# Sums of a fast matrix product kept in PSUM and read between their terms, in the feed-forward layer of a decoder step

## The chip, the cores and the metric

The kernel runs on one core of a Trainium2 chip. The metric is the device time of one execution in microseconds (us). A core has five engines that run their own instruction streams and wait for each other by semaphores: TensorE (PE, matrix products into PSUM), VectorE (DVE), ScalarE (ACT), GpSimd (POOL) and SyncE (SP, which here issues loads).

## The reference, cut to what matters

One decoder layer on 512 prompt rows and 8 x 4 sample rows, 544 token columns in all, in float32. Only its last part is touched by the change:

```python
x += SwiGLU(RMSNorm(x))              # D_MODEL 2048, FFN_HIDDEN 5632
def swiglu(h, w_gate, w_up, w_down):
    return (jax.nn.silu(h @ w_gate) * (h @ w_up)) @ w_down
y = rmsnorm(x, norm_final_w)
```

Ahead of it stand the token mixer (a recurrent group and a sliding-window attention) and a memory cross-attention, which take the first 1137 us of the span and are the same before and after.

## The kernel before

**Units.** The three feed-forward products are made in units by a fast scheme with 7 products in place of 8. Weights and activations are cut into 2 x 2 blocks; `unit` (L1642) loads the four weight blocks A11, A21, A12, A22 by two DMAs of 1 MB on SP (tile `sraw`) and POOL makes three combinations S1, S2, S3 and later a fourth (tile `scomb`, 3 buffers, `comb` at L1655). The 7 products come in the order B11, B21, T2, T1, T3, B22, T4, named by the activation block that each multiplies. There are 44 units of gate and up (22 pairs; the weight block is 8 row tiles by one column tile) and then 20 units of w_down: 5 blocks `b` of hidden rows by 4 groups `o4` of output columns. The last 4 of the 44 row tiles of hidden values go through the plain product `gemm` at the end.

**Products.** Each product is 24 matmuls of 128 x 272 (L1692): the weights are split in a high part `shi` and a low part `slo`, the activations too, and high x high, high x low, low x high are added in PSUM. `split_w2` (L1634) makes the parts: ACT copies the source to a PSUM tile `h2` (rounded; L1638; "h" in the rows), ACT casts the source to `shi` (L1639), and DVE subtracts `h2` from the source into `slo` (L1640). `shi` and `slo` have two buffers each, so those of product q+2 can be written only when PE has ended product q; `h2` has one buffer (two banks), so a copy waits for the DVE subtraction of the product before. The 24 matmuls need `slo` first at their third.

**Results.** Each product has a PSUM tile of its own (`s_ps`, pool `ps_acc`, 2 buffers of 2 banks each; T1's is in `ps_s`), and `done` reads it out:

- gate and up (`gu_unit`, L1701): ACT copies B11's result twice (L1712, L1713), and DVE adds and subtracts the other six into the four result blocks (8 instructions of 272 columns, L611 and L1699), with four multiplications by the norm factor in a gate unit (L1706).
- w_down (`down_unit`, L1875): B11, T2, T1 and T3 go into sums of their own in SBUF (`sums`): ACT copies in block 0 (L1884), DVE adds from block 1 on; B21, B22 and T4 are added by DVE straight to `x`. In the last block 32 more additions of 544 columns (`x_sum`, L1862, its instruction at L1870) bring the sums into `x`: those of one `o4` in the unit after it, from the unit's hook, and those of the last in its own `done`, partly on POOL.

**Activation operands.** The split operands of the w_down blocks are made beside the units: `Block.early` (in the unit before the block, o4 = 3) and `Block.late` (in the block's first unit, o4 = 0). POOL forms the differences (L1756), ACT casts the high part (L606), DVE subtracts it for the low part (L607; two inputs in SBUF, 1088 columns). In the last block's second unit `last_h` splits the 4 row tiles that are left (L607, 544 columns).

**Order.** Within one engine the instructions stand in the order that the program's builder gives them when it places them by its own estimate of readiness, so the order of a line in the source is not always the order on the engine: `h2` and `shi` of one product, which the source writes in that order, can stand either way round on ACT.

Of the kernel before, what the change touches and what calls it, by code (L numbers as in the profile page):

```python
# [19 lines left out]
P = 128  # L20
# [24 lines left out]
def hybrid_step(ctx: ExitStack, tc: tile.TileContext, a):  # L45
# [13 lines left out]
    ps_s = pool("ps_s", bufs=2, space=PSUM)  # L59
# [4 lines left out]
    def ps(name, tag="t"):  # L64
        return (ps_s if tag == "s" else ps_to[0]).tile([P, 512], F32, tag=tag, name=name)
# [1156 lines left out]
    def norm_rows(out, sums, tag="t"):  # L1222

        for (b, e), s in zip(HALF, sums):
            pt = ps("nr_ps", tag)[:, : TT // 2]
# [404 lines left out]
    to_ctx.close()  # L1630
    ph_ctx = ctx.enter_context(ExitStack())
    ps_h = ph_ctx.enter_context(tc.tile_pool(name="ps_h", bufs=1, space=PSUM))

# [8 lines left out]
    def unit(w1, w2, n0, m, ops, done, hook=None, loaded=None, summed=None):  # L1642
# [23 lines left out]
        if summed:  # L1666
            with tc.issue_after(last.ins):
                summed()
        for i, (q, src) in enumerate((
# [3 lines left out]
            if src is None:  # L1673
                src, _ = comb(A12, S2, SPLIT)
# [21 lines left out]
            done(q, accs if q == "T1" else acc[:, :m, :HT])  # L1696
# [4 lines left out]
    def gu_unit(w, n0, c, f, *more):  # L1701
# [6 lines left out]
        def done(q, acc):  # L1708
            c11, c12, c21, c22 = (c[:, i, t] for i in range(2) for t in (T0, T1))
            acc = acc[0] if q == "T1" else acc[:, 0]  # L1710
# [23 lines left out]
        held = []  # L1734
        unit(*w, n0, 1, fops.get, done, *more)


# [69 lines left out]
    for j in range(FF // P // 2):  # L1807
# [10 lines left out]
        def first_gate(i):  # L1818
            if i == 2:
                norm_rows(R3, S3, "s")  # L1820
# [24 lines left out]
    AG = ((xq, "q0"), (xq, "q1"), (ws, "gu"))  # L1845
    AQ = ("B11", "T2", "T1", "T3")
    sums = []

    def load_x():
        for o4 in range(KD // 4):  # L1850
            X[o4] = group(*XG[o4], f"x3{o4}")
            dma(X[o4], x3_d[:, 4 * o4 : 4 * o4 + 4])
            if o4 < 3:
                t = group(*AG[o4], "sums", F32, (P, 4, 2, HT))
                sums.append({q: t[:, i] for i, q in enumerate(AQ)})
            else:
                tags = ((post, "sqt"), (post, "sqt"), (post, "nv"), (big, "R"))
                sums.append({
                    q: p.tile([P, 2, HT], F32, tag=t, name="sums", bufs=1 + (t == "sqt"))
                    for q, (p, t) in zip(AQ, tags)  # L1860
                })

    def x_sum(o4, n, eng):
        x = X[o4]
        x11, x12, x21, x22 = (x[:, 2 * i : 2 * i + 2, t] for i in range(2) for t in (T0, T1))
        p1, p6, p5, p7 = (sums[o4][q] for q in AQ)
        y, z = (
            (x11, p1), (p6, p1), (x12, p6), (x12, p5), (x22, p5), (p7, p6), (x21, p7), (x22, p7),
        )[n]
# [238 lines left out]
```

## Time and profile before

| | us |
|---|---|
| median of 3 runs | 2612.46 (2611.51 to 2615.15) |
| the profiled execution | 2610.72 |
| its span | 2608.9 |
| PE busy in the span | 2520.0 (97%) |
| DVE, ACT, POOL busy | 1688.9, 1583.8, 1083.2 |

The span is what the profile's views cover; the profiled execution's time is 1.82 us more. A row of the timeline gives start, duration, engine, line, operation, the tiles out<-in, and in square brackets how long the engine had been idle and what released it. Matmuls overlap: one of 272 columns shows about 0.29 us and the next starts about 0.126 us later. A PEclk of 1.00 is the full granted clock.

### The profile page before, as it was taken

The page shows a single profiled execution, that of the slowest core. Times are in us where ns is not written, and L with a number is a line of the kernel's source. Part 1 is how long each engine was busy: PE and PEld are TensorE (multiplying, and loading weights), DVE is VectorE, ACT ScalarE, POOL GpSimd, SP SyncE. Part 2 cuts the span into 40 slices and gives each one's busy share as a digit, 9 for nine tenths or more (in the row PEclk, how much of TensorE's full clock was granted, in tenths as well). Part 3 has the DMA queues.
Part 4 walks back from the last instruction along what each step waited for, and adds up shares of the span by engine and source line. Part 5 has one row for each costly group of instructions (what it writes and reads, how often), then busy time and mean ns, then how long its engine had stood idle before and what let it go on. Part 6 is the DMA issues. An engine that isn't in the chain of part 4 may idle for free.

```text
span 2608.9 us, 48418 instructions
## 1 busy us (share of the span) xinstructions
PE 2520.0 (97%) x19679; PEld 2452.7 (94%) x19679; DVE 1688.9 (65%) x2575; ACT 1583.8 (61%) x2177; POOL 1083.2 (42%) x623
## 2 busy tenths in 40 slices
PE   8999899999999999989999999999999999999997
PEld 7999899998998998879999999999999999999997
DVE  5555555556558796597666665666656666767897
ACT  5344223333326785467777777777777778777757
POOL 4201222122024741265554555555555556665632
PEclk9999999999999999999999999999999999999999
DMA  7322323544523416622333333333333453333325
GB/s 227 85 74 81 84 82 91 150 147 127 184 78 100 131 61 186 202 96 94 116 115 123 117 118 115 106 115 106 115 106 115 145 204 132 115 115 132 115 68 164
DMA packets 287391, 315.48 MB, mean 121 GB/s; under 512 B 9731, under 2 KB 239443, under 8 KB 284320
## 3 DMA queue, kind: packets, MB, share of 16 engines
q1 hardware_dynamic: 273024, 264.80, 32.0%
q0 software_dynamic: 14144, 47.58, 5.5%
q8 instruction: 155, 2.54, 0.4%
q14 instruction: 68, 0.56, 0.1%
HBM read 278.28 MB, written 33.64 MB: 120 GB/s over the span
## 4 chain that ended last, share of the span: by engine, by line
PE 82%; DVE 7%; ACT 3%; DMA 3%; issue 2%; POOL 2%; SPq 0%; ACTq 0%; POOLq 0%; DVEq 0%
PE s_ps L1692 49%; PE in_ps L345 17%; PE o_ps L1145 4%; PE ha_ps L929 2%; PE d_ps L154 2%; DVE wlo L132 1%; PE mq_ps L1440 1%; PE o_ps L509 1%; PE s_ps L471 1%; PE mkv_ps L684 1%; DVE slo L1640 1%; DMA wraw<-in_w_in_dram 1%; PE in_ps L154 1%; ACT shi L1639 1%; PE t_ps L489 0%
## 5 line engine op out<-in xcount | busy, mean ns | idle before, releaser
L1640 DVE TENSOR_TENSOR slo<-scomb,h 128x1024 fp32r<-128x1024 f32 x256 | 311.6, 1217 | 132.0 <-PE s_ps L1692 110.6
L131 ACT CAST whi<-wraw 128x1024 fp32r<-128x1024 f32 (+1 forms) x204 | 169.7, 846 | 357.6 <-PE in_ps L345 286.4
L1638 ACT CAST h<-scomb 128x1024 fp32r<-128x1024 f32 x256 | 260.9, 1019 | 130.8 <-DVE slo L1640 118.5
L1657 POOL TENSOR_TENSOR scomb<-sraw 128x1024 f32<-128x1024 f32 x128 | 316.0, 2469 | 9.2 <-DVE slo L1640 4.4
L1639 ACT CAST shi<-scomb 128x1024 fp32r<-128x1024 f32 x256 | 269.8, 1054 | 53.5 <-PE s_ps L1692 49.9
L1657 POOL TENSOR_TENSOR scomb<-sraw,scomb 128x1024 f32<-128x1024 f32 x64 | 166.5, 2602 | 287.5 <-DVE slo L1640 242.0
L345 PE MATMUL in_ps<-xh,whi 128*128 128x272 f32 x1280 | 276.2, 297 | 0.3 <-ACT whi L131 0.3
L345 PE MATMUL in_ps<-xl,whi 128*128 128x272 f32 x1280 | 274.9, 295 | 0.0
L345 PE MATMUL in_ps<-xh,wlo 128*128 128x272 f32 x1280 | 272.4, 294 | 0.6 <-DVE wlo L132 0.5
L1692 PE MATMUL s_ps<-T,shi 128*128 128x272 f32 x1408 | 269.3, 288 | 2.6 <-ACT shi L1639 2.6
L132 DVE TENSOR_TENSOR wlo<-wraw,whi 128x1024 fp32r<-128x1024 f32 (+1 forms) x204 | 208.6, 1035 | 95.0 <-ACT whi L131 90.8
L1638 ACT CAST h<-sraw 128x1024 fp32r<-128x1024 f32 x192 | 195.3, 1017 | 121.5 <-DVE slo L1640 121.2
L611 DVE TENSOR_TENSOR gu<-gu,s_ps 128x272 f32<-128x272 f32 x264 | 111.6, 437 | 237.5 <-PE s_ps L1692 237.5
L1692 PE MATMUL s_ps<-dT,shi 128*128 128x272 f32 x1280 | 243.9, 289 | 0.0
L1640 DVE TENSOR_TENSOR slo<-sraw,h 128x1024 fp32r<-128x1024 f32 x192 | 233.2, 1214 | 10.7 <-ACT h L1638 7.3
L1639 ACT CAST shi<-sraw 128x1024 fp32r<-128x1024 f32 x192 | 201.5, 1050 | 57.8 <-PE s_ps L1692 49.3
L1692 PEld LDWEIGHTS s_ps<-T,shi 128*128 128x128 f32 x1408 | 221.2, 188 | 3.0 <-ACT shi L1639 2.8
L345 PEld LDWEIGHTS in_ps<-xh,wlo 128*128 128x128 f32 x1280 | 202.5, 189 | 6.3 <-issue 4.8
L345 PEld LDWEIGHTS in_ps<-xh,whi 128*128 128x128 f32 x1280 | 202.0, 189 | 6.0 <-issue 4.3
L345 PEld LDWEIGHTS in_ps<-xl,whi 128*128 128x128 f32 x1280 | 202.4, 189 | 5.0 <-issue 4.4
L1692 PE MATMUL s_ps<-T,slo 128*128 128x272 f32 x704 | 203.6, 289 | 1.3 <-DVE slo L1640 1.3
L1692 PEld LDWEIGHTS s_ps<-dT,shi 128*128 128x128 f32 x1280 | 201.1, 188 | 0.0
(521 smaller groups left out, 7375.1 us busy)
## 6 DMA issues: line engine op xcount, KB each, us to landing
sraw<-in_w_gate_dram SPq DMA_DIRECT2D x44, 1024.0 KB, 5.3
sraw<-in_w_up_dram SPq DMA_DIRECT2D x44, 1024.0 KB, 5.3
wraw<-in_w_in_dram SPq DMA_DIRECT2D x84, 512.0 KB, 3.9
sraw<-in_w_down_dram SPq DMA_DIRECT2D x40, 1024.0 KB, 5.4
oraw<-in_w_out_dram SPq DMA_DIRECT2D x32, 512.0 KB, 4.4
h_d<-gu POOLq DMA_DIRECT2D x22, 544.0 KB, 3.7
wraw<-in_w_mk_dram SPq DMA_DIRECT2D x16, 512.0 KB, 3.7
wraw<-in_w_mv_dram SPq DMA_DIRECT2D x16, 512.0 KB, 4.0
```

What stands on the lines that cost most here:

```text
L131: nc.scalar.copy(hi[:, s], raw[:, s])
L132: nc.vector.tensor_tensor(lo[:, s], raw[:, s], hi[:, s].bitcast(F32), SPLIT)
L154: nc.tensor.matmul(acc[:, i, : e - b], wt, xt[:, b:e], start=first, stop=last)
L345: nc.tensor.matmul(acc[:, i, : e - b], wt, xt[:, b:e], start=j + at == 0, stop=j == KD - 1 and at == 2,)
L611: nc.vector.tensor_tensor(out, x, y, ALU.add)
L929: nc.tensor.matmul(pairs(pa[:, b], hb), kp[:, c], odd(qq[:, c], hb), start=True, stop=True)
L1145: nc.tensor.matmul(acc[:, p, :HT], wt[:, k, s], xt_[:, k], start=first and k + at == 0, stop=k == DN - 1 and at == 2, skip_group_check=True,)
L1638: first = nc.scalar.copy(h2, src)
L1639: nc.scalar.copy(hi, src)
L1640: return first, nc.vector.tensor_tensor(lo, src, h2.bitcast(F32), SPLIT)
L1657: return t, nc.gpsimd.tensor_tensor(t, x, y, op)
L1692: nc.tensor.matmul(accs[p], wt[:, k, s], xt_[:, k], start=k + at == 0, stop=k == n - 1 and at == 2,)
```

## The change

- The terms of a unit's sums are added up in PSUM. The first bank pair takes B11, then T2, T3 and T4 on top; the second takes B21, then (started anew) T1, then B22 on top. `done` reads the pair after each product, so it reads P(B11), P(B11)+P(T2) and so on, and the next product into that pair waits for that read. Pairs are taken in turn from three: two of `ps_acc`, one of a new pool `ps_x`; `ps_s` is closed while the layer runs.
- Gate and up: B22's weight combination changes sign (`neg`); ACT makes one copy per unit (T1's, times -1; in up units T4's too), DVE 5 reads and up to 4 multiplications.
- w_down: each of the 7 products is one DVE addition of 544 columns straight to `x`. The `sums` tiles, ACT's copies of block 0 and all 32 `x_sum` additions are gone.
- `norm_rows` of the first up unit uses an `h2` tile; `ps_s` is made again for the final norm.

```diff
-    def unit(w1, w2, n0, m, ops, done, hook=None, loaded=None, summed=None):
+    def unit(w1, w2, n0, m, ops, done, neg, hook=None, loaded=None, summed=None):
...
+        banks = ffn_acc(), ffn_acc()
...
-                src, _ = comb(A12, S2, SPLIT)
+                src, _ = comb(S2, A12, SPLIT) if neg else comb(A12, S2, SPLIT)
...
-            if q == "T1":
-                accs = [ps("s5_ps", "s")[:, :HT] for p in range(m)]
-            else:
-                acc = acc_tile("s_ps")
-                accs = [acc[:, p, :HT] for p in range(m)]
+            acc = banks[int(q in ("B21", "T1", "B22"))]
...
-                            accs[p], wt[:, k, s], xt_[:, k],
-                            start=k + at == 0, stop=k == n - 1 and at == 2,
+                            acc[:, p, :HT], wt[:, k, s], xt_[:, k],
+                            start=k + at == 0 and q in ("B11", "B21", "T1"),
+                            stop=k == n - 1 and at == 2, skip_group_check=True,
...
             if q == "B11":
-                nc.scalar.copy(c11, acc)
-                nc.scalar.copy(c12, acc)
+                nc.vector.tensor_copy(c11, acc)
             elif q == "B21":
                 add(c11, c11, acc)
+                last(c11, T0)
             elif q == "T2":
-                add(c12, c12, acc)
+                nc.vector.tensor_copy(c12, acc)
             elif q == "T1":
-                held.append(acc)
-                last(c11, T0)
+                nc.scalar.activation(c22, acc, AF.Copy, scale=-1.0)
             elif q == "T3":
-                add(c21, c12, acc)
-                add(c22, c12, acc)
-                less(c22, c22, held[0])
+                add(c22, c22, acc)
+                last(c22, T1)
             elif q == "B22":
-                add(c12, c12, acc)
-                less(c12, c12, held[0])
-                last(c22, T1)
+                less(c12, c12, acc)
+                last(c12, T1)
+            elif f is None:
+                nc.scalar.copy(c21, acc)
             else:
-                last(c12, T1)
-                add(c21, c21, acc)
-                last(c21, T0)
...
+                nc.vector.tensor_tensor(c21, acc, f[:, T0], ALU.mult)
...
-            y = dict(sums[o4], B21=x11, B22=x12, T4=x21)[q]
-            for y, acc in zip((y[:, 0], y[:, 1]), acc) if q == "T1" else ((y, acc),):
-                if b == 0 and q in AQ:
-                    nc.scalar.copy(y, acc)
-                else:
-                    add(y, y, acc)
+            y = dict(B11=x11, B21=x11, T2=x12, T1=x22, T3=x22, B22=x12, T4=x21)[q]
+            add(y, y, acc)
...
-            elif o4 and b == NBLK - 1:
-                def late(i, o4=o4):
-                    x_sums(o4 - 1, i)
-                    if o4 == 1:
-                        last_h(i)
-
-                more = late, None
+            elif o4 == 1 and b == NBLK - 1:
+                more = last_h, None
```

The order of instructions moves with it. On ACT, in the second unit of w_down's block 1 (a plain unit, with no operands to make beside it), the four products T2, T1, T3 and B22 stand like this in the kernel before (`h_` is the copy to `h2`; in brackets the semaphores that the instruction waits for):

```order
L1638 CAST h_24390<-scomb 128x1024 [waits DVE_49,Pool_49]
L1639 CAST shi<-scomb 128x1024 [waits PE_49,Activation_49]
L1638 CAST h_24422<-scomb 128x1024 [waits DVE_49]
L1639 CAST shi<-scomb 128x1024 [waits PE_49,Activation_49]
L1638 CAST h_24456<-scomb 128x1024 [waits DVE_49,Pool_49]
L1639 CAST shi<-scomb 128x1024 [waits PE_49,Activation_49]
L1638 CAST h_24490<-scomb 128x1024 [waits DVE_49,Pool_49]
L1639 CAST shi<-scomb 128x1024 [waits PE_49,Activation_49]
```

and in the changed one, where L1652 is the cast to `shi` and L1651 the copy:

```order
L1652 CAST shi<-scomb 128x1024 [waits PE_49,Activation_49,Pool_49]
L1651 CAST h_23979<-scomb 128x1024 [waits DVE_49]
L1652 CAST shi<-scomb 128x1024 [waits PE_49,Activation_49]
L1651 CAST h_24010<-scomb 128x1024 [waits DVE_49]
L1652 CAST shi<-scomb 128x1024 [waits PE_49,Activation_49,Pool_49]
L1651 CAST h_24041<-scomb 128x1024 [waits DVE_49]
L1652 CAST shi<-scomb 128x1024 [waits PE_49,Pool_49]
L1651 CAST h_24074<-scomb 128x1024 [waits DVE_49]
```

The copy stood ahead of its product's cast and now stands behind it; the cast, which waits for PE, is now the first of the two. The cast stands first in all 20 units of w_down; before, it did so throughout in the last two only, and in none of the fifth to the eighteenth. In gate and up the copy stays ahead.

On DVE, in the first unit of block 1, where the operands of T1 and T3 are split (L607, now L608) beside the products, before:

```order
L611 TENSOR_TENSOR sums<-sums,s_ps 128x544
L1640 TENSOR_TENSOR slo<-scomb,h_24140 128x1024
L607 TENSOR_TENSOR dT_24144<-t_23822,dT_24144 128x1088
L611 TENSOR_TENSOR x_23068<-x_23068,s_ps 128x2x272
L1640 TENSOR_TENSOR slo<-scomb,h_24175 128x1024
L607 TENSOR_TENSOR dT_24179<-hA,dT_24179 128x1088
L611 TENSOR_TENSOR sums<-sums,s_ps 128x544
L1640 TENSOR_TENSOR slo<-scomb,h_24212 128x1024
```

and in the changed kernel:

```order
L612 TENSOR_TENSOR x_22699<-x_22699,s_ps 128x2x272
L608 TENSOR_TENSOR dT_23706<-hA,dT_23706 128x1088
L1653 TENSOR_TENSOR slo<-scomb,h_23736 128x1024
L612 TENSOR_TENSOR x_22699<-x_22699,s_ps 128x2x272
L608 TENSOR_TENSOR dT_23740<-t_23425,dT_23740 128x1088
L1653 TENSOR_TENSOR slo<-scomb,h_23770 128x1024
L612 TENSOR_TENSOR x_22699<-x_22699,s_ps 128x2x272
L608 TENSOR_TENSOR dT_23774<-hA,dT_23774 128x1088
L1653 TENSOR_TENSOR slo<-scomb,h_23804 128x1024
```

A product's addition (L611, now L612) stood behind the operand's split and the subtraction for `slo` followed it; now the addition, which waits for PE, comes first, the split behind it, and `slo` last.

On POOL the fourth combination of the last up unit now stands ahead of the difference of hA and hB that belongs to the first block; before it stood behind it. SP's order is unchanged, and PE's nearly so.

## Rows read from the trace of the kernel before

**Rows 1.** sections 1 and 5 of the page: count, busy us, mean ns
```profile
PE 2520.0 (97%) x19679; PEld 2452.7 (94%) x19679; DVE 1688.9 (65%) x2575; ACT 1583.8 (61%) x2177; POOL 1083.2 (42%) x623
...
L611 DVE TENSOR_TENSOR gu<-gu,s_ps 128x272 f32<-128x272 f32 x264 | 111.6, 437 | 237.5 <-PE s_ps L1692 237.5
```

**Rows 2.** windows: stretch, its length, busy us of each engine (x instructions), PEclk
```profile
1250.00:2050.00 800.00, 800.00 (x6352) 800.00 (x6351) 486.36 (x682) 580.50 (x623) 423.50 (x189) 1.00 0.34 113
2092.22:2183.69 91.47, 87.11 (x675) 85.19 (x674) 56.89 (x50) 72.29 (x84) 54.97 (x23) 1.00 0.44 154
2183.69:2459.13 275.44, 275.44 (x2187) 275.44 (x2186) 205.22 (x222) 210.76 (x209) 170.82 (x65) 1.00 0.37 125
2459.13:2533.60 74.47, 67.11 (x506) 65.44 (x505) 69.05 (x77) 41.87 (x45) 28.59 (x12) 0.98 0.21 71
```

**Rows 3.** starved matmuls, timeline of PE: start, us, engine, line, [idle before <-releaser]
```profile
1154.92 0.60 PE L1692 MATMUL s_ps<-T2h,shi 128*128 128x272 f32 x1 [2.25 <-ACT gu L1713]
...
1189.95 0.39 PE L1692 MATMUL s_ps<-T,shi 128*128 128x272 f32 x1 [2.61 <-ACT shi L1639]
...
1194.98 0.39 PE L1692 MATMUL s_ps<-B,slo 128*128 128x272 f32 x1 [1.49 <-DVE slo L1640]
...
2081.91 0.39 PE L1692 MATMUL s_ps<-T,slo 128*128 128x272 f32 x1 [0.69 <-DVE slo L1640]
...
2086.32 0.40 PE L1692 MATMUL s_ps<-B,slo 128*128 128x272 f32 x1 [1.13 <-DVE slo L1640]
...
2177.52 0.39 PE L1692 MATMUL s_ps<-dB,shi 128*128 128x272 f32 x1 [0.26 <-ACT shi L1639]
...
2478.17 0.39 PE L1692 MATMUL s_ps<-dB,slo 128*128 128x272 f32 x1 [3.52 <-DVE slo L1640]
```

**Rows 4.** timeline, ACT and DVE, in a plain unit of w_down (block 1)
```profile
2228.18 1.02 ACT L1638 CAST h<-scomb 128x1024 fp32r<-128x1024 f32 x1 [0.96 <-DVE slo L1640]
2229.19 1.06 ACT L1639 CAST shi<-scomb 128x1024 fp32r<-128x1024 f32 x1
...
2229.27 0.72 DVE L611 TENSOR_TENSOR sums<-sums,s_ps 128x544 f32<-128x544 f32 x1 [1.17 <-PE s_ps L1692]
2229.91 1.21 DVE L1640 TENSOR_TENSOR slo<-scomb,h 128x1024 fp32r<-128x1024 f32 x1
```

**Rows 5.** timeline, PE, ACT and DVE, in the last block's third unit
```profile
2485.59 0.41 PE L1692 MATMUL s_ps<-dB,shi 128*128 128x272 f32 x2
...
2491.88 0.41 PE L1692 MATMUL s_ps<-dT,shi 128*128 128x272 f32 x2
2492.34 0.39 PE L1692 MATMUL s_ps<-dT,slo 128*128 128x272 f32 x1
...
2489.00 1.06 ACT L1639 CAST shi<-scomb 128x1024 fp32r<-128x1024 f32 x1 [1.33 <-PE s_ps L1692]
...
2491.07 1.22 DVE L1640 TENSOR_TENSOR slo<-scomb,h 128x1024 fp32r<-128x1024 f32 x1 [0.88 <-ACT h L1638]
```

**Rows 6.** timeline, DVE and POOL, in the first unit of blocks 1 and 0
```profile
2182.46 2.40 POOL L1657 TENSOR_TENSOR scomb<-sraw 128x1024 f32<-128x1024 f32 x1
2192.14 3.44 POOL L1657 TENSOR_TENSOR scomb<-sraw,scomb 128x1024 f32<-128x1024 f32 x1 [7.27 <-ACT dT L606]
...
2192.01 1.29 DVE L607 TENSOR_TENSOR dT<-hA,dT 128x1088 fp32r<-128x1088 f32 x1
...
2108.18 3.14 DVE L607 TENSOR_TENSOR dB<-hB,dB 128x1088 fp32r<-128x1088 f32 x1
```

**Rows 7.** timeline, POOL and ACT, in the fourth unit of block 0
```profile
2169.16 2.57 POOL L1756 TENSOR_TENSOR hA<-hA 128x1088 f32<-128x1088 f32 x1 [5.22 <-DVE dB L607]
...
2175.18 1.02 ACT L1638 CAST h<-scomb 128x1024 fp32r<-128x1024 f32 x1 [1.52 <-POOL scomb L1657]
```

**Rows 8.** timeline, DVE, in the last block's second unit
```profile
2471.77 5.22 DVE L607 TENSOR_TENSOR hl<-hr,hh 128x544 fp32r<-128x544 f32 x2
...
2478.67 2.55 DVE L1870 TENSOR_TENSOR sums<-sums 128x544 f32<-128x544 f32 x1
```

More of the change, by code (lines that the diff above doesn't have):

```diff
@@ L58, in hybrid_step @@
     ps_acc = pool("ps_acc", bufs=2, space=PSUM)
-    ps_s = pool("ps_s", bufs=2, space=PSUM)
+    s_ctx = ctx.enter_context(ExitStack())
+    ps_s = [s_ctx.enter_context(tc.tile_pool(name="ps_s", bufs=2, space=PSUM))]
     dpool = pool("dpool", space=DRAM)
@@ L1224, in norm_rows @@
         for (b, e), s in zip(HALF, sums):
-            pt = ps("nr_ps", tag)[:, : TT // 2]
+            if tag == "h2":
+                pt = ps_h.tile([P, 2, 512], F32, tag="h2", name="nr_ps")[:, 0, : TT // 2]
+            else:
+                pt = ps("nr_ps", tag)[:, : TT // 2]
             n = s.shape[1]
@@ L1630, in hybrid_step, with ffn_acc @@
     to_ctx.close()
+    s_ctx.close()
     ph_ctx = ctx.enter_context(ExitStack())
     ps_h = ph_ctx.enter_context(tc.tile_pool(name="ps_h", bufs=1, space=PSUM))
+    ps_x = ph_ctx.enter_context(tc.tile_pool(name="ps_x", bufs=1, space=PSUM))
+    accs_made = count()
+    def ffn_acc():
+        if next(accs_made) % 3 == 2:
+            return ps_x.tile([P, 2, 512], F32, tag="x", name="s_ps")
+        return acc_tile("s_ps")
     def split_w2(hi, lo, src):
@@ L1692, in unit @@
                         nc.tensor.matmul(
-                            accs[p], wt[:, k, s], xt_[:, k],
-                            start=k + at == 0, stop=k == n - 1 and at == 2,
+                            acc[:, p, :HT], wt[:, k, s], xt_[:, k],
+                            start=k + at == 0 and q in ("B11", "B21", "T1"),
+                            stop=k == n - 1 and at == 2, skip_group_check=True,
                         )
-            done(q, accs if q == "T1" else acc[:, :m, :HT])
+            done(q, acc[:, :m, :HT])
     def less(out, x, y):
@@ L1709, in done @@
             c11, c12, c21, c22 = (c[:, i, t] for i in range(2) for t in (T0, T1))
-            acc = acc[0] if q == "T1" else acc[:, 0]
+            acc = acc[:, 0]
             if q == "B11":
-                nc.scalar.copy(c11, acc)
-                nc.scalar.copy(c12, acc)
+                nc.vector.tensor_copy(c11, acc)
             elif q == "B21":
                 add(c11, c11, acc)
+                last(c11, T0)
             elif q == "T2":
-                add(c12, c12, acc)
+                nc.vector.tensor_copy(c12, acc)
             elif q == "T1":
-                held.append(acc)
-                last(c11, T0)
+                nc.scalar.activation(c22, acc, AF.Copy, scale=-1.0)
             elif q == "T3":
-                add(c21, c12, acc)
-                add(c22, c12, acc)
-                less(c22, c22, held[0])
+                add(c22, c22, acc)
+                last(c22, T1)
             elif q == "B22":
-                add(c12, c12, acc)
-                less(c12, c12, held[0])
-                last(c22, T1)
-            else:
-                last(c12, T1)
-                add(c21, c21, acc)
-                last(c21, T0)
-        held = []
-        unit(*w, n0, 1, fops.get, done, *more)
+                less(c12, c12, acc)
+                last(c12, T1)
+            elif f is None:
+                nc.scalar.copy(c21, acc)
+            else:
+                nc.vector.tensor_tensor(c21, acc, f[:, T0], ALU.mult)
+        unit(*w, n0, 1, fops.get, done, True, *more)
     RING = [(xnp, t) for t in ("xl0", "xh1", "xl1", "xh3", "xl3", "xh2", "xl2")]
@@ L1852, in load_x @@
             dma(X[o4], x3_d[:, 4 * o4 : 4 * o4 + 4])
-            if o4 < 3:
-                t = group(*AG[o4], "sums", F32, (P, 4, 2, HT))
-                sums.append({q: t[:, i] for i, q in enumerate(AQ)})
-            else:
[L1857 to L1869, printed above, removed]
-        eng.tensor_tensor(y, y, z, ALU.add)
-    def x_sums(o4, i):
-        for n in (i,) if i < 6 else (6, 7):
-            x_sum(o4, n, nc.vector)
     def down_unit(b, o4, blk, *more):
@@ L1880, in done @@
             x11, x12, x21, x22 = (x[:, 2 * i : 2 * i + 2, t] for i in range(2) for t in (T0, T1))
-            y = dict(sums[o4], B21=x11, B22=x12, T4=x21)[q]
-            for y, acc in zip((y[:, 0], y[:, 1]), acc) if q == "T1" else ((y, acc),):
-                if b == 0 and q in AQ:
-                    nc.scalar.copy(y, acc)
-                else:
-                    add(y, y, acc)
-            if b == NBLK - 1 and o4 == KD // 4 - 1:
-                for n in dict(B21=(0,), T2=(1,), T1=(2, 4), T3=(5,), B22=(3, 7), T4=(6,)).get(q, ()):
-                    x_sum(o4, n, nc.gpsimd if n in (0, 4, 7) else nc.vector)
+            y = dict(B11=x11, B21=x11, T2=x12, T1=x22, T3=x22, B22=x12, T4=x21)[q]
+            add(y, y, acc)
         f0 = blk.f0
@@ L1895, in down_unit @@
         )
-        unit(w1, w2, o4 * 4 * P, 2, blk.ops.get, done, *more)
+        unit(w1, w2, o4 * 4 * P, 2, blk.ops.get, done, False, *more)
     f1 = 2 * DN * NBLK
```

8 lines of the change are left out of this document (3 added, 5 removed).

## The prediction

> **What bounds the kernel now.** The page's first section comes first: PE is busy for 97% of the span, DVE for 65%, ACT for 61% [rows 1]. So a change in DVE's or ACT's work is worth only what PE waits for it, and the next view is the windows, stage by stage. In gate and up PE is busy for 800.00 of 800 us with 6352 matmuls, 0.126 us each [rows 2]; a product of 24 is then 3.03 us and a unit of 7 products 21.18 us. The 13 units from w_down's fifth on take 275.44 us against 13 x 21.18 = 275.3, so nothing is to be won there either. The first four units take 91.47 against 84.7, 6.8 over; the last three 74.47 against 63.5, 10.9 over [rows 2]. All that the change can gain in w_down is therefore 17.7 us, and the first 13 units after the fourth can only lose. Third, the starved matmuls in PE's timeline [rows 3]: those at 1154.92, 1189.95 and 1194.98 belong to the entry into gate and up (2.25 + 2.61 + 1.49 = 6.35 us), those at 2081.91 and 2086.32 to the last up unit (0.69 + 1.13 = 1.8), the one at 2478.17 to the last block (3.52). Last, the timeline of ACT and DVE shows why the 13 units lose nothing.
>
> That is the reading on which the forecast hangs. In a plain unit of block 1, ACT copies a product's source to `h2` at 2228.18 and casts it to `shi` at 2229.19; DVE adds the product that just ended at 2229.27 and subtracts for `slo` at 2229.91 [rows 4]. Only the cast has to wait until PE has ended the product two before; the copy was done ahead of that moment, so `slo` is ready at 2231.12, some 1.9 us after the product's end, where the next product takes 3.03. The last block's third unit shows the same work with ACT's cast ahead of the copy: the cast starts at 2489.00, released by PE, the copy after it, and DVE's `slo` only at 2491.07, to 2492.29; the product that needs it starts at 2491.88 and its first low-part matmul runs at 2492.34, 0.46 after, where 0.25 is the normal distance [rows 5]. From the start of one product at 2485.59 to the start of the next but one at 2491.88 are 6.29 us instead of 6.05: **0.12 us per product, 0.8 per unit**. The chain is cast 0.95 (the part of its 1.06 before the next instruction starts), copy 1.0, subtraction 1.22, and the hand-overs between them: 3.3 us against a product's 3.03 plus 0.25.
>
> **The change, part by part.**
>
> *Gate and up, steady units: 0.* The copy stays ahead of the cast. DVE loses 3 of its 8 additions, gains 2 plain reads; ACT loses a copy. PE was fully busy, so the lighter load buys nothing. What is added is a wait: T2 waits for the read of B11, T1 for B21's, T3 for T2's, B22 for T1's, T4 for T3's. Each read has one whole product, 3.03 us, of room. On DVE it may stand behind one `slo` of 1.21 and takes 0.44 (the 272-column addition [rows 1]; twice that with the multiplication): 2.1 at most. ACT's one copy stands behind a cast of 0.95. So it is hidden by the product between; with that cover gone each wait would show whole.
>
> *Entry into gate and up: +1.3* (from -1 to +4). The operands are split there beside the first units, DVE's queue is full, and now T2 waits for DVE's read of B11 instead of ACT's copy; by the order on DVE that read stands behind T1's `slo` and ends 0.75 us after the 1154.92 of before. Later the `slo` of T3 stands behind the norm's chain as it did, and the casts before it: I get 2.0 + 3.5 for the pair that was 2.61 + 1.49, or 1.4 more; together 2.1, of which I take off 0.8 because a later T2 lets the parts behind it catch up.
>
> *Last up unit: -1.8.* On POOL the fourth combination comes ahead of the difference of hA and hB. The waits at 2081.91 and 2086.32 came from that queue [rows 3].
>
> *w_down.* Gone are the ACT copies of block 0 and the 32 `x_sum` additions; all seven additions per unit stay on DVE as before (0.72). What counts is the order: the cast now leads in all 20 units. I go through them against a unit of 21.18.
>
> - 10 plain units at the 0.8 of above: 8.0. Two of them are the last two units, which so far lose 5.6 together: of the 10.9 of the last three I put 5.3 on the second unit, 3.52 of it starved in one piece [rows 3].
> - First units of blocks 1 to 4 (four): the addition now comes first, then the operand's split, then `slo`. T1's `slo` ends 3.35 us after B21's end and frees the buffer for POOL's fourth combination, which takes 2.40 [rows 6]. Before, DVE's split of 1.29 was issued 0.13 ahead of it and POOL waited, 3.44 in place of 2.40 [rows 6]; now the addition stands between, POOL goes first and the split waits: combination done at +5.8, split at +7.1, T3's `slo` at +8.3, where its low part is due at +6.5: 1.8 us. Splits behind a POOL instruction are dear elsewhere too: 3.14 in block 0 [rows 6]. For the two splits of B22 and T4 I take 0.6 each, a third of such a delay of 1.85. With 0.2 of chain: 3.2 per unit, 12.8.
> - Block 0's first unit, on which I put 5.4 of block 0's 6.8 because its operands come late, starts with the same late operands and gets the new order: 6.5.
> - Fourth units of blocks 0 to 3 (four): the addition goes ahead of the split of B11's operand, POOL's next difference waits for that split, as it did for 5.22 us before, and ACT's copy at 2175.18 waited 1.52 for the fourth combination behind it, which starved PE for 0.26 at 2177.52 [rows 7, 3]. Now the cast comes ahead of the copy (0.95 more) and the chain begins 0.4 later: 1.6. With 0.5 for the next difference in POOL's queue and 0.5 of chain: 2.6, in all 10.4.
> - The last block's second unit: two splits of 544 columns took 5.22 beside POOL and starved PE for 3.52 [rows 8, 3]; the `x_sum` of 0.8 ahead of them goes, the rest stays: 4.5 where 5.3 were lost.
>
> Together 8.0 + 12.8 + 6.5 + 10.4 + 4.5 = 42.2 us over, against 17.7: **+24.5**. Final product and norm: 0, the same instructions on banks made anew.
>
> The sum: 2610.72 (the profiled execution, span 2608.9) + 0 + 1.3 - 1.8 + 24.5 = 2634.7. The median shown, 2612.46, lies 1.7 above that execution, well inside what is forecast; I take **2634.5**. Low end: chain only every second product (0.4 per unit), late and fourth units free of extra, entry -1: about 2607. High end: 5 per late unit, 4 per fourth, entry +4: about 2652.
>
> [...] PE's steady stage shows 800.00 busy of 800 us with results read from one bank pair while PE writes another [rows 2]; no row has a reader and PE taking turns within one sum. [...]
>
> **The rivals.**
>
> *Only the chain costs.* Splits and combinations may fall so that late and fourth units lose no more than plain ones: PE that lags a little gives POOL and DVE more time. For it: before, the first unit of block 1 ran without a stall although POOL took 3.44. Against: that order had the split first. Then 18 units x 0.8 = 14.4, block 0's first 4.0, the splits of 544 columns 4.5: 22.9, +5.2, with -1.8 and +1.3 about **2615.4**.
>
> *Faster.* The cast-first order is hidden, because nothing delays DVE where `x_sum` delayed it in the rows that I read for 0.8: an `x_sum` of two SBUF inputs took 2.55 beside POOL [rows 8]. Then the last two units give back 5.6, the second 0.8, the last up unit 1.8, and the entry takes 1.3: **2603.8**. It decides if cast, copy and subtraction end within 3.28 us of a product's end. Against: in the rows at 2489 to 2492 no `x_sum` stands between the copy's end and the subtraction [rows 5].
>
> *Gate and up lose too.* If reads in the in-order queues of DVE or ACT come later than a product's room, each of 42 units loses, say, 0.5, one read's 0.44 and a hand-over: 21 us more, **2655**. Against: the 2.1 of 3.03 above.
>
> **How the numbers follow.** The forecast 0.55, only the chain 0.24, faster 0.08, gate and up 0.13. About 0.2% (5.2 us) is what a measurement of this kernel can tell from no change. The forecast and the third rival lie wholly above it; of "only the chain" I put 0.14 within and 0.09 above. Faster 0.09, same 0.14, slower 0.77. The range runs from 2612 to 2654: it leaves out the faster rival, half of the chain's low side and the far side of the third.
>
> **What would show it.** In the changed profile: plain units of w_down at 22.0 instead of 21.18, with ACT's cast released by PE and `slo` idle behind ACT's copy; T3's split stretched beside POOL's combination in the first units; gate and up still fully busy from 1250 to 2050; no waits left in the last up unit. Idle matmuls in gate and up, or plain units at 21.18, would prove me wrong.

## The result, and the profile after

The changed kernel takes 2637.47 us (median of 4 runs, 2635.39 to 2639.32), the kernel before 2611.99 in the same comparison: a ratio of 1.0095, 95% interval 1.0082 to 1.0107. It is slower by about 25 us.

The profiled execution is 2639.28 us with a span of 2637.5. The page's first section [rows 1 before]:

```profile
PE 2541.8 (96%) x19679; PEld 2461.7 (93%) x19679; DVE 1648.0 (62%) x2414; ACT 1569.6 (60%) x2136; POOL 1076.1 (41%) x620
```

PE is busy 21.8 us longer with the same 19679 matmuls: one that waited shows a longer duration (0.39 in place of 0.29 in rows below), so short waits are inside the busy time, and so are the slower matmuls of the stretches at a lower clock (below). DVE is busy 41 us less and ACT 14 us less. So the engines that were relieved did less work, and PE waited more. Where, the windows say [rows 2 before]: gate and up; w_down's block 0; the 13 units from its fifth on; the last three units. Columns are length, then busy us of PE, PEld, DVE, ACT, POOL, PEclk, DMA share, GB/s.

```profile
1250.00:2050.00 800.00, 800.00 (x6352) 800.00 (x6351) 455.00 (x567) 580.49 (x604) 423.52 (x190) 1.00 0.34 112
2094.02:2188.68 94.66, 89.44 (x675) 85.83 (x673) 67.62 (x64) 62.66 (x64) 58.37 (x24) 1.00 0.43 154
2188.68:2489.81 301.13, 289.98 (x2187) 279.01 (x2185) 214.47 (x209) 206.22 (x208) 169.57 (x65) 1.00 0.34 115
2489.81:2561.83 72.02, 68.97 (x506) 67.10 (x505) 45.07 (x46) 42.26 (x45) 21.89 (x9) 0.95 0.23 75
```

Gate and up is as full as before: 800.00 of 800 us, 6352 matmuls, while DVE's busy time there fell from 486.36 to 455.00 for nothing. The 13 units that lost nothing before (275.44) take 301.13 us. Block 0 takes 94.7 in place of 91.5, and the last three units 72.0 in place of 74.5.

The whole splits at three rows of PE's timeline: the layer's first matmul, w_down's first, and the first of the plain product behind it.

| us | before | after | difference |
|---|---|---|---|
| up to the layer's first matmul (same program) | 1143.66 | 1141.18 | -2.5 |
| gate and up, with its entry and last unit | 948.56 | 952.84 | +4.3 |
| w_down's 20 units | 441.42 | 467.81 | +26.4 |
| plain product, final norm | 75.26 | 75.67 | +0.4 |

The first line is the spread of the program ahead: in the ten profiles of this study it lies between 1137.2 and 1146.3, and the runs of the kernel before lie between 2603.9 and 2615.8. A few us can therefore be told by stage, not by the whole, and that is how the runs below are read.

**The granted clock.** PEclk is 0.95 in the last three units, and was 0.98 before. The loss lies in single stretches: the last block's second unit after, and the same unit before (columns: length, busy us of PE, PEclk, DMA share, GB/s), and PE at the end of its wait after:

```profile
2508.40:2515.10 6.70, 6.06 (x26) 0.50 0.37 116
2479.10:2482.30 3.20, 3.20 (x16) 0.50 0.00 0
```

```profile
2509.04 0.60 PE L1705 MATMUL s_ps<-dB,slo 128*128 128x272 f32 x1 [3.04 <-DVE slo L1653]
```

PE stands still for 3.04 us up to 2509.04 (before: 3.52 up to 2478.17, rows 3), and in these stretches the granted clock is 0.50 in place of 1.00. Three matmuls take 0.68 us there (2509.43 to 2510.11) and 0.38 at a clock of 1.00 (2516.14 to 2516.52), so the longer stretch costs some 3 us and the shorter some 1.5 (estimates from these rows). The entry into gate and up has three such stretches after (at 1146.5, 1190.9 and 1208.0), one before (at 1154.7). They do not come with every wait: gate and up's third unit takes 25.29 us with one (after) and 23.77 without (experiment 1), with the same wait of 2.33 and 2.34 in it. Units in which PE starves can therefore differ from run to run, here by 1.5 us and, by the estimate for the longer stretch, by 3; the plain units and the first units of blocks 1 to 4 after have no such stretch.

A plain unit of block 1, PE, ACT and DVE [rows 4 and 5 before]:

```profile
2238.38 0.41 PE L1705 MATMUL s_ps<-dB,shi 128*128 128x272 f32 x2
2238.68 0.39 PE L1705 MATMUL s_ps<-dB,slo 128*128 128x272 f32 x1
2238.91 0.41 PE L1705 MATMUL s_ps<-dB,shi 128*128 128x272 f32 x2
```

```profile
2235.41 1.05 ACT L1652 CAST shi<-sraw 128x1024 fp32r<-128x1024 f32 x1 [1.21 <-issue]
2236.36 1.01 ACT L1651 CAST h<-sraw 128x1024 fp32r<-128x1024 f32 x1
2238.53 1.05 ACT L1652 CAST shi<-scomb 128x1024 fp32r<-128x1024 f32 x1 [1.16 <-PE s_ps L1705]
```

```profile
2235.49 0.72 DVE L612 TENSOR_TENSOR x<-x,s_ps 128x544 f32<-128x544 f32 x1
2237.40 1.22 DVE L1653 TENSOR_TENSOR slo<-sraw,h 128x1024 fp32r<-128x1024 f32 x1 [1.19 <-ACT h L1651]
```

The cast starts at 2235.41, 0.12 after the next product's first matmul (its row names no releaser; the unit's next cast, at 2238.53, is put down to PE). The copy follows at 2236.36, and DVE, idle for 1.19 behind ACT's copy, subtracts from 2237.40 to 2238.62. The product that needs it starts at 2238.38; its third matmul runs at 2238.68, 0.30 after the first instead of 0.25, and the products of the unit take 3.05 to 3.30 us in place of 3.03. That is the chain of rows 5, now in every unit: from one unit's first matmul to the next, the ten plain units take 22.05 to 22.21 us, on average 22.10, 0.92 over.

The first unit of block 2, DVE, POOL and PE around T3's operand [rows 6 before]:

```profile
2289.64 1.22 DVE L1653 TENSOR_TENSOR slo<-scomb,h 128x1024 fp32r<-128x1024 f32 x1
2291.02 0.72 DVE L612 TENSOR_TENSOR x<-x,s_ps 128x544 f32<-128x544 f32 x1 [0.17 <-PE s_ps L1705]
2291.66 2.89 DVE L608 TENSOR_TENSOR dT<-hA,dT 128x1088 fp32r<-128x1088 f32 x1
2294.47 1.21 DVE L1653 TENSOR_TENSOR slo<-scomb,h 128x1024 fp32r<-128x1024 f32 x1
```

```profile
2291.00 2.40 POOL L1673 TENSOR_TENSOR scomb<-sraw,scomb 128x1024 f32<-128x1024 f32 x1 [9.41 <-DVE slo L1653]
```

```profile
2294.61 0.39 PE L1705 MATMUL s_ps<-dT,shi 128*128 128x272 f32 x1 [0.47 <-DVE dT L608]
2295.74 0.40 PE L1705 MATMUL s_ps<-dT,slo 128*128 128x272 f32 x1 [0.74 <-DVE slo L1653]
```

T1's `slo` ends at 2290.85; POOL's fourth combination starts at 2291.00 and takes its plain 2.40; DVE's addition goes first, and its split, issued at 2291.66, lasts 2.89 where it took 1.29 before. T3 starts 0.47 late for its operand and is held 0.74 more for `slo`. The first units of blocks 1 to 4 take 24.2 to 24.6 us, 3.1 over.

### The profile page after: what moved, and what is told of

Same layout as the page of the kernel before. It is cut to its first block, busy times and chain, and to the rows that moved or that the text cites. A ratio compares the mean times of both kernels' runs of the same rounds, so it can differ in the third digit from the quotient of the medians.

```text
span 2637.5 us, 48262 instructions
## 1 busy us (share of the span) xinstructions
PE 2541.8 (96%) x19679; PEld 2461.7 (93%) x19679; DVE 1648.0 (62%) x2414; ACT 1569.6 (60%) x2136; POOL 1076.1 (41%) x620
## 5 line engine op out<-in xcount | busy, mean ns | idle before, releaser
L1673 POOL TENSOR_TENSOR scomb<-scomb,sraw 128x1024 f32<-128x1024 f32 x108 | 266.9, 2471 | 197.4 <-DVE slo L1653 180.5
L1652 ACT CAST shi<-scomb 128x1024 fp32r<-128x1024 f32 x256 | 269.2, 1052 | 122.4 <-PE s_ps L1705 108.3
L1651 ACT CAST h<-scomb 128x1024 fp32r<-128x1024 f32 x256 | 259.6, 1014 | 101.1 <-DVE slo L1653 98.9
L1652 ACT CAST shi<-sraw 128x1024 fp32r<-128x1024 f32 x192 | 201.4, 1049 | 121.4 <-PE s_ps L1705 81.6
L1651 ACT CAST h<-sraw 128x1024 fp32r<-128x1024 f32 x192 | 195.0, 1016 | 66.3 <-DVE slo L1653 64.1
L1705 PE MATMUL s_ps<-dT,slo 128*128 128x272 f32 x640 | 191.8, 300 | 6.7 <-DVE slo L1653 5.8
```

Source lines behind the costliest of these rows:

```text
L1651: first = nc.scalar.copy(h2, src)
L1652: nc.scalar.copy(hi, src)
L1673: return t, nc.gpsimd.tensor_tensor(t, x, y, op)
L1705: nc.tensor.matmul(acc[:, p, :HT], wt[:, k, s], xt_[:, k], start=k + at == 0 and q in ("B11", "B21", "T1"), stop=k == n - 1 and at == 2, s ...
```

## The experiments

Stage times are taken at the same three matmuls of PE's timeline as in the table; a unit's time runs from its first matmul in PE's timeline (where the operands of B11 and B21 follow those of T4) to the next unit's.

**1. The copy put back ahead of the cast** (w_down only):

```diff
         first = nc.scalar.copy(h2, src)
-        nc.scalar.copy(hi, src)
+        if h_first:
+            with tc.issue_after(first.ins):
+                nc.scalar.copy(hi, src)
+        else:
+            nc.scalar.copy(hi, src)
...
-            ins = split_w2(hi, lo, src)
+            ins = split_w2(hi, lo, src, not neg)
```

(`neg` is false in w_down only.)

> The changed kernel with one order put back: in w_down each product's copy to h2 stands ahead of its cast to shi on ACT (in gate and up nothing changes); DVE's splits of the operands then also stand ahead of the additions again. If the order is what costs: plain units of w_down go from 22.1 to 21.2 us, the first units of blocks 1 to 4 from 24.2 to 21.2-21.5, the fourth units from 23.8 to 21.2-21.8, the last two units to 21.2; the stage from the first to the last unit takes 430 to 437 us instead of 467, the whole about 2604 to 2608. If the waits of one product for the read of an earlier sum in the same banks are what costs (rival), the units stay at 22.1 and the time within 3 us of 2637.

Measured: 2597.12 us (2594.73 to 2603.93), ratio to the kernel before 0.9945, interval 0.9926 to 0.9964. w_down takes 428.0 us. Both lie below what I expected (2604 to 2608, 430 to 437): the last block's second unit (22.3 in place of 27.9) and block 0's first (24.3 in place of 26.5), which the expectation doesn't name, came down too. The windows of the 13 units and of the last two (each begins 0.76 us ahead of its units), and ACT and DVE in a plain unit:

```profile
2186.44:2461.87 275.43, 275.43 (x2187) 275.43 (x2185) 205.19 (x208) 211.06 (x208) 170.87 (x65) 1.00 0.37 125
2484.20:2526.57 42.37, 42.37 (x338) 42.37 (x337) 25.41 (x28) 27.34 (x27) 12.00 (x5) 1.00 0.17 60
```

```profile
2231.70 1.02 ACT L1651 CAST h<-scomb 128x1024 fp32r<-128x1024 f32 x1 [0.96 <-DVE slo L1657]
2232.72 1.05 ACT L1654 CAST shi<-scomb 128x1024 fp32r<-128x1024 f32 x1
```

```profile
2232.79 0.72 DVE L612 TENSOR_TENSOR x<-x,s_ps 128x544 f32<-128x544 f32 x1 [1.18 <-PE s_ps L1709]
2233.43 1.22 DVE L1657 TENSOR_TENSOR slo<-scomb,h 128x1024 fp32r<-128x1024 f32 x1
```

All 13 units, first and fourth ones among them, are back at 21.18 (PE busy for 275.43 of 275.43), with the same banks, reads and waits as in the changed kernel. DVE's `slo` follows its addition at once, since the copy is long done. In w_down the loss was in the order. Two orders changed here, ACT's by the edit, and DVE's, in which the builder put the splits ahead of the additions again; experiments 3 and 4 part them. In w_down the waits of a product for the read of an earlier sum cost PE something in one place only, block 0's first unit, where T2 waits for the addition of B11. That addition stands in DVE's queue behind a split that takes 3.50 beside POOL:

```profile
2102.87 3.50 DVE L608 TENSOR_TENSOR dT<-hA,dT 128x1088 fp32r<-128x1088 f32 x1
2106.29 0.71 DVE L612 TENSOR_TENSOR x<-x,s_ps 128x544 f32<-128x544 f32 x1
```

```profile
2107.15 0.48 PE L1709 MATMUL s_ps<-dT,shi 128*128 128x272 f32 x2 [1.02 <-DVE x L612]
```

The entry into gate and up has the other such wait, T2's for DVE's read of B11: 3.06 us in this run, 1.75 in the changed kernel, where the kernel before waited 2.25 for ACT's copies [rows 3].

**2. The cast put first in the kernel before:**

```diff
-        first = nc.scalar.copy(h2, src)
-        nc.scalar.copy(hi, src)
+        if shi_first:
+            cast = nc.scalar.copy(hi, src)
+            with tc.issue_after(cast.ins):
+                first = nc.scalar.copy(h2, src)
+        else:
+            first = nc.scalar.copy(h2, src)
+            nc.scalar.copy(hi, src)
...
-            ins = split_w2(hi, lo, src)
+            ins = split_w2(hi, lo, src, m == 2)
```

(`m` is 2 in w_down only.)

> The kernel before with one order changed: in w_down each product's cast to shi stands ahead of its copy to h2 on ACT; sums, banks and x_sum additions stay as they were. If the order is what costs: plain units go from 21.18 to 22.0-22.1 us, first units of blocks 1 to 4 to about 24, and the whole becomes 20 to 28 us longer, 2631 to 2640. If the loss needs the sums in PSUM (rival), the time stays within 3 us of 2611.

Measured: 2646.74 us (2644.95 to 2653.88), ratio 1.0136 (1.0113 to 1.0159). Sums in SBUF, and yet w_down takes 481.2 us, 39.8 more; I had expected 20 to 28. Plain units of blocks 1 to 4 take 22.05, first units 24.8 to 25.6, fourth units 23.8 to 24.5. PE's waits in w_down:

```profile
PE s_ps L1697 <- DVE slo L1645: 28.5, 33, 3.0
PE s_ps L1697 <- DVE dT L607: 1.9, 4, 0.5
PE s_ps L1697 <- ACT shi L1639: 0.8, 1, 0.8
```

Against 10.5 us for `slo` in 8 waits before, 28.5 in 33. The excess over the forecast is in the fourth units, which I had left out (2.6 to 2.8 each, 10.6 together), in the first ones (3.8 each where I had 3), and in block 0's second and third, 23.6 with ACT's copies of the sums in the chain. Three stretches at the lower clock, about 1.5 us each, are in it; w_down had one before. The third unit of the last block, which had the cast first before, stays at 23.46.

Here too a second order moved: with the cast first the builder put most of DVE's additions ahead of the operand splits in the first and fourth units, as in the changed kernel. In block 2's first unit, DVE and POOL:

```profile
2292.72 0.72 DVE L611 TENSOR_TENSOR sums<-sums,s_ps 128x544 f32<-128x544 f32 x1 [0.17 <-PE s_ps L1697]
2293.36 2.89 DVE L607 TENSOR_TENSOR dT<-hA,dT 128x1088 fp32r<-128x1088 f32 x1
```

```profile
2292.69 2.41 POOL L1662 TENSOR_TENSOR scomb<-sraw,scomb 128x1024 f32<-128x1024 f32 x1 [9.38 <-DVE slo L1645]
```

So the two orders together cost this in either kernel, without any sum in PSUM; the plain units, which have no split, show the cast's share alone.

**3. DVE's split put back ahead of the addition**, the cast still first (the source now calls the read of a product after the next product's operand split and ties it behind that split on DVE):

```diff
-                    hook(i)
+                    made = hook(i)
+                if late_done and made is not None:
+                    with tc.issue_after(made.ins):
+                        late_done()
+                    late_done = None
...
-            done(q, acc[:, :m, :HT])
+            if m == 2:
+                late_done = lambda q=q, acc=acc: done(q, acc[:, :m, :HT])
+            else:
+                done(q, acc[:, :m, :HT])
```

> The changed kernel with DVE's split of an operand put back ahead of the product's addition in the first and fourth units of w_down; the cast stays ahead of the copy. If POOL's combination getting in ahead of the split is the cost there: the first units of blocks 1 to 4 go from 24.2 to 22.1-22.5 us, the fourth units of blocks 0 to 3 from 23.8 to 22.3-23, plain units stay at 22.1; the whole 10 to 14 us shorter, 2623 to 2628. If the order of cast and copy alone makes those units slow (rival): no change, 2635 to 2639.

Measured: 2629.21 us (2626.7 to 2632.19), ratio 1.0064 (1.0049 to 1.0079); w_down 459.8, 8.0 less than in the changed kernel. First units 22.4 to 22.7 (from 24.2), fourth units 23.1 to 23.3 (from 23.8), plain units 22.0 to 22.3. In the first unit of block 2:

```profile
2289.68 1.28 DVE L608 TENSOR_TENSOR dT<-hA,dT 128x1088 fp32r<-128x1088 f32 x1
```

```profile
2289.91 3.33 POOL L1673 TENSOR_TENSOR scomb<-sraw,scomb 128x1024 f32<-128x1024 f32 x1 [9.39 <-DVE slo L1653]
```

DVE's split is issued 0.23 ahead and keeps its 1.28; POOL pays, 3.33 instead of 2.40. For the first units the forecast held; for the fourth it was too large (0.7 each, I had 0.8 to 1.5), and block 0's first unit (27.4 from 26.5) and the last block's second (28.3 from 27.9) rose, so the stage fell by 8 and not by 10 to 14. Block 0's first unit has a stretch at the lower clock here and none in the changed kernel; the 1.5 us of that are more than the 0.9 by which it rose.

**4. The addition held ahead of the split, the copy first:**

```diff
-                    hook(i)
+                    with ExitStack() as behind:
+                        if m == 2 and i:
+                            behind.enter_context(tc.issue_after(sums_made[-1]))
+                        hook(i)
```

(`sums_made` holds w_down's additions; edit 1 is in this kernel too.)

> The copy ahead of the cast in w_down, but DVE's operand splits held behind the product's addition. If POOL's combination gets in ahead of the split whatever ACT's order is: first units of blocks 1 to 4 23 to 24 us (T3 late by 1.5 to 2), fourth units 21.5 to 23, plain units 21.2; the whole 10 to 16 us above copy first, 2606 to 2613. If those units lost only by the cast (rival): all at 21.2 to 21.4, the whole 2596 to 2600.

Measured: 2621.35 us (2617.38 to 2624.35), ratio 1.0041 (1.0027 to 1.0055); w_down 450.4, 22.4 above copy first. Plain units 21.18, fourth units 22.55, first units 23.91. Their T3:

```profile
2280.02 2.99 DVE L608 TENSOR_TENSOR dT<-hA,dT 128x1088 fp32r<-128x1088 f32 x1
```

```profile
2279.45 2.41 POOL L1678 TENSOR_TENSOR scomb<-sraw,scomb 128x1024 f32<-128x1024 f32 x1 [8.02 <-ACT dT L607]
```

```profile
2283.06 0.39 PE L1713 MATMUL s_ps<-dT,shi 128*128 128x272 f32 x1 [0.56 <-DVE dT L608]
2284.19 0.39 PE L1713 MATMUL s_ps<-dT,slo 128*128 128x272 f32 x1 [0.74 <-DVE slo L1658]
```

The same picture as in the changed kernel: POOL 0.57 ahead, DVE's split 2.99 long, PE starved twice. With the copy first, the split's place alone is worth 2.7 us in a first unit, 1.4 in a fourth, and 4.4 in the last block's second unit (26.7 against 22.3). The stage's 22.4 is above the 16 that I gave as the top because that last unit and block 0's first (26.0 against 24.3) weren't counted.

The four kernels with the sums in PSUM make a table of w_down's time:

| us | split ahead of the addition | addition ahead of the split |
|---|---|---|
| copy ahead of the cast | 428.0 | 450.4 |
| cast ahead of the copy | 459.8 | 467.8 (the change) |

The cast's order costs 17 to 32 us, the split's 8 to 22; together they cost 39.8, less than the 31.8 and 22.4 that each costs alone. My reading, which no run tests, is that a PE that is late for one leaves time for the other. Of these totals 450.4 holds one short stretch at the lower clock, 459.8 a short and a long one, 467.8 a long one and 428.0 none: by the estimates above 1.5, 4.5 and 3 us, which changes the prices but not the order of the four.

**5. The norm's row sums in another bank pair:**

```diff
-        for (b, e), s in zip(HALF, sums):
+        both = acc_tile("nr_ps") if tag == "h2" else None
+        for i, ((b, e), s) in enumerate(zip(HALF, sums)):
...
-                pt = ps_h.tile([P, 2, 512], F32, tag="h2", name="nr_ps")[:, 0, : TT // 2]
+                pt = both[:, i, : TT // 2]
```

> The changed kernel with the row sums of the norm (nr_ps, in the first up unit) in a bank pair of ps_acc instead of the one h2 buffer. If sharing h2 is what holds up the entry: the third unit's 25.3 us becomes 21.2 and the first four units together about 4 us shorter (101.5 instead of 105.6), the whole 2633 to 2635. If the entry is slow because T2, T1 and T3 wait for reads behind DVE's queue (rival): the first four units stay within 1 us of 105.6.

**6. The first pair's product behind the next unit's split:** an issue-order edge on DVE, so that the two multiplications of the first gate and up pair (L1849) stand behind the `slo` of the next unit's B21.

```diff
+            n0 = len(splits)
             gu_unit(wg, 2 * j * P, g, R3)
+            if j == 1:
+                for p in first_prods:
+                    tc.add_manual_dep(
+                        p.ins, splits[n0 + 1].name,
...
```

> The changed kernel with the one edit that DVE's product of the first gate and up pair stands behind its split of the next unit's B21. If that queue is the wait: the third unit goes from 25.3 (24 in other runs) to 21.2 us, the rest stays, first four units about 102 instead of 104.3 to 105.9; w_down unchanged at 466 to 468. Rival: the wait moves on, within 1 us of before.

Both are about the entry, so the changed kernel's rows come first, PE's waits there [rows 3 before] and DVE's queue ahead of them:

```profile
1183.82 0.39 PE L1705 MATMUL s_ps<-T,shi 128*128 128x272 f32 x1 [1.54 <-ACT shi L1652]
...
1190.32 0.39 PE L1705 MATMUL s_ps<-T,slo 128*128 128x272 f32 x1 [3.21 <-DVE slo L1653]
...
1206.53 0.39 PE L1705 MATMUL s_ps<-B21h,slo 128*128 128x272 f32 x1 [2.33 <-DVE slo L1653]
```

```profile
1177.95 0.44 DVE L1234 TENSOR_SCALAR nv<-nr_ps 128x272 f32<-128x272 f32 x1 [0.48 <-PE nr_ps L1232]
...
1180.67 0.43 DVE L1234 TENSOR_SCALAR nv<-nr_ps 128x272 f32<-128x272 f32 x1
...
1182.51 1.22 DVE L1653 TENSOR_TENSOR slo<-scomb,h 128x1024 fp32r<-128x1024 f32 x1
...
1184.12 2.51 DVE L88 SCALAR_TENSOR_TENSOR nt<-nt,nv 128x272 f32<-128x272 f32 x1
1186.66 2.47 DVE L89 SCALAR_TENSOR_TENSOR R<-nt,R 128x272 f32<-128x272 f32 x1
1189.06 1.21 DVE L1653 TENSOR_TENSOR slo<-scomb,h 128x1024 fp32r<-128x1024 f32 x1
...
1203.98 1.36 DVE L1849 TENSOR_TENSOR gu<-gu 128x544 f32<-128x544 f32 x2 [4.48 <-POOL gu L1826]
1205.26 1.22 DVE L1653 TENSOR_TENSOR slo<-sraw,h 128x1024 fp32r<-128x1024 f32 x1
```

The row sums hold `h2` until DVE has read them (1177.95, 1180.67); only then come the copies for T1 and T3, and the `slo` of T3 is queued behind two steps of the norm that take 2.51 and 2.47 beside POOL. PE stands still for 3.21. Later the product of the first pair (1203.98) waits 4.48 for POOL and keeps B21's `slo` behind it: 2.33 at 1206.53.

Measured, norm in another bank: median 2640.43 (2633.13 to 2642.2), by the whole not to be told from 2637.47; by stage clear: gate and up 948.02 in place of 952.84, its first four units 101.2 in place of 106.0, the second unit's T3 3.9 us long in place of 8.0. The gain came in the second unit (26.2 in place of 30.0) and not, as I had expected, in the third: that one takes 24.0, its wait at B21 stays (2.46), and only its stretch at the lower clock is gone. Measured, product late: 2636.75 (2632.66 to 2641.51), gate and up 949.95, the third unit 21.4 in place of 25.3, w_down unchanged at 467.07; the other waits stay:

```profile
1181.05 0.40 PE L1707 MATMUL s_ps<-T,shi 128*128 128x272 f32 x1 [1.55 <-ACT shi L1653]
...
1187.55 0.60 PE L1707 MATMUL s_ps<-T,slo 128*128 128x272 f32 x1 [3.21 <-DVE slo L1654]
```

The first four units take 103.1: the second grew by 1.1 at the same two waits, while the granted clock was 0.50 from 1186.6 to 1193.3, 6.7 us, where the changed kernel has 3.4. So the two are separate, 4.8 and 2.9 us by stage, and the wait did not move on. Both sums hold differences in the stretches at the lower clock; by PE's waits alone the second unit loses 2.5 us less with the norm in another bank (2.27 in place of 4.75), and the third 2.3 less with the product late.

**7. Copy first with both of these:** edits 1, 5 and 6 together.

> The changed kernel with the copy ahead of the cast in w_down, the norm's row sums in ps_acc, and the product of the first gate and up pair behind DVE's split of the next unit's B21. Copy first alone: 2597. Of the entry's 105.7 us norm_bank took off 4.5; if the third unit's wait of 2.3 to 2.5 us before B21's slo is DVE standing in its queue behind that product, the third unit falls from 24 to 21.2 and the first four together to 98 to 99, as in the kernel before; the whole 2588 to 2593. If the wait only moves to the next product (rival), the four stay at 101 and the whole at 2593 to 2596.

Measured: 2592.84 us (5 runs, 2589.41 to 2594.82), ratio to the kernel before 0.9933 (0.9919 to 0.9946). Gate and up 945.59 us, first four units 98.8; w_down 430.27, nearly all of its 6.7 over in block 0's first unit (5.4) and the last block's second (1.2). It beats both kernels, the one before by 0.67% and the changed one by 45 us (2637.47, from its own comparison).

**8. The kernel before with the copy first in all units:** edit 1 in the kernel before (with `m == 2`).

> The kernel before with the copy ahead of the cast in all units of w_down (it was not in the first unit and the last two). Tells what the change is worth at equal order. If the last two units lost by the cast: 21.2 to 22 us each instead of 23.1 and 23.8, the whole 4 to 5 us shorter, 2606 to 2609, still above copy first in the changed kernel by about 10. If they lost by the x_sum additions (rival): they stay at 22.5 or more and the whole at 2609 to 2612.

Measured: 2604.08 us (10 runs, 2597.94 to 2608.45), ratio 0.9976 (0.9964 to 0.9988); w_down is 3.7 us shorter in the profiles. The last two units take 21.6 and 21.7 in place of 23.5 and 24.6: most of that was the cast. What is left over 21.2, 0.4 to 0.5 each, goes with `x_sum`: without it, in experiment 1, both units take 21.2. The two work together, as the third unit shows: 0.9 over with the cast first alone (changed kernel), 0.4 with `x_sum` alone, 2.3 with both. The second unit of the last block rose from 26.5 to 27.6, at the same wait in one piece but a longer stretch at the lower clock:

```profile
2475.75 0.60 PE L1696 MATMUL s_ps<-dB,slo 128*128 128x272 f32 x1 [3.52 <-DVE slo L1644]
```

With the sums in PSUM and no `x_sum` the same unit takes 22.3 (experiment 1). At equal order, then, the change's w_down is worth 437.8 - 428.0 = 9.8 us, or 7.5 by experiment 7, which has the same w_down (430.3), and its gate and up costs 4.7 (953.05 against 948.36). Some 4.5 us of the 9.8 are stretches at the lower clock that this run has in block 0's first and the last block's second unit and experiment 1 has not.

## Why the prediction was right

The forecast of 2634.5 lies 3.0 under the median, and the mechanism is the one it named. That it came so close is in part luck. The stages that it added up (+24.0) took 31.1 us more in the two profiles (4.3 + 26.4 + 0.4), 7.1 above the sum; the program ahead happened to be 2.5 shorter in the second one, and the medians differ by 25.5 where the two profiles differ by 28.6. By its steps:

- *Plain units, 0.8 each:* 0.92. Shown by experiments 1 and 2: ACT's order brings it and takes it away, in either kernel; experiment 4 has it at 21.18 with DVE's order as in the change.
- *First units of blocks 1 to 4, 3.2 each:* 3.1, T3's split behind POOL's combination as worked out (held 1.6 us longer; the stall 0.47 + 0.74 beside the chain). In block 2's first unit T3's product takes 4.76 in place of 3.03, 1.7 where 1.8 was forecast; B22 and T4 lose 0.4 each and not 0.6, the chain 0.55 and not 0.2. Experiments 3 and 4 show the place of the split to be worth 1.8 to 2.7 of it.
- *Fourth units, 2.6 each:* 2.6 (23.77 to 23.88). Only 0.7 of it goes with the split's place when the cast is first (1.4 when the copy is). The rest I put down, without a run of its own, to the chain and to a cast that waits 2.99 for POOL's combination (block 1's fourth unit, at 2271.94). Right in sum, and the shares were guesses.
- *Block 0's first unit, 6.5:* 5.3, as before the change (5.4): the new order cost nothing there that this profile shows. *The last block's second, 4.5:* 6.7, the wrong way: it lost 5.3 before. It is still starved for 3.04 in one piece, and the stretch at the lower clock behind that, which the step did not price, is twice as long as before. This unit takes 22.3 only with the copy ahead, the splits ahead and no `x_sum` together (experiments 1 and 7); in all other runs it takes 26.5 to 28.3.
- w_down in all: +26.4 measured, +24.5 forecast; the plain units (+1.2) and the last block's second (+2.2) came out dearer, block 0's first (-1.2) cheaper.
- *Steady gate and up, 0:* 800.00 of 800 again, so the rival in which it loses 0.5 per unit is out. *Last up unit, -1.8:* it takes 21.3 us in place of 23.5.
- *Entry, +1.3 (to +4):* the step that was furthest off, and outside its own range: the first four units take 106.0 in place of 99.5, 6.5 more. The parts that it priced came out near: T2 starts 0.9 later after the layer's first matmul than before (0.75 forecast), and the second unit's two waits are 1.54 + 3.21 (2.0 + 3.5 forecast, 2.61 + 1.49 before). It left out the third unit's wait of 2.33, for B21's `slo` behind DVE's multiplications of the first pair (2.9 by stage, experiment 6), and two more stretches at the lower clock, some 3 us. It also never costed the move of `nr_ps` to the single `h2` buffer, an edit that I had described (4.8 by stage, experiment 5).
- *"Only the chain costs"* fell with the first units at 24.2. *"Faster"* fell with the plain units; experiment 8 shows that most of what the unit of rows 5 lost went with the cast.

What stays open is why the builder turned ACT's order round; no run tells which edit did it. DVE's order followed ACT's in both directions (experiments 1 and 2).

## What to carry to other kernels

Where one of two instructions in an engine's queue has to wait for a long event and the other has not, the one that need not wait goes first: here a copy of 1 us behind a cast, and a split behind an addition, took 40 us together (467.8 against 428.0 in w_down). After an edit that relieves engines, compare the order of every engine's instructions, also far from the edit, before crediting the work removed: DVE lost 41 us of work and the kernel became slower. Cost a shared buffer like a wait: a tile that borrows the only buffer of a chain holds up the chain (4.8 us in gate and up, experiment 5). And look at PEclk before comparing units in which PE starved (25.29 and 23.77 us with the same wait of 2.3).

## What the runs showed of the hardware

Two things came out cleaner than I had expected. Where DVE's split for T3, a subtraction with both inputs in SBUF, met POOL's combination in block 2's first unit, the one issued first kept its time and the other took longer: in experiment 3 DVE first by 0.23, 1.28 and 3.33 (POOL's plain time is 2.40); in experiment 4 POOL first by 0.57, 2.99 and 2.41 (DVE's plain time is 1.28). In both the later one ended within 0.15 us of the other's end plus its own plain time, as if it had waited for the other. And reading a sum out of PSUM between two products that add to it cost PE nothing measurable in experiment 1's plain stage: 275.43 us of 275.43 with seven reads in each unit, four of them between two products of one sum, and one product of 3.03 us of room for each read. Where the reader was late, PE waited for it: 1.02 us in block 0's first unit (experiment 1), 1.75 (the changed kernel) and 3.06 (experiment 1) in the entry.
